# Smaller loads among the last 48 rows, and a hand-written list of operations for the last 24

## The chip, the cores and the metric

The kernel runs on one core of a Trainium2 chip. The metric is the device time of one execution in microseconds (us), as the median of several. A profile of one execution shows what each engine did; its span is some 2 us shorter than the device time. In the profiles PE is TensorE's matmul, PEld its weight load, DVE VectorE, ACT ScalarE, POOL GpSimd, SP the engine that issues the loads.

## The reference

```python
def setup_inputs():
    batch, seq, dim = 32, 512, 1024
    return {"x": np.abs(np.random.randn(batch, seq, dim)).astype(np.float32) + 1e-6}

def reference(x):
    return np.sum(1.0 / x, axis=-1).astype(np.float32)
```

That is 16384 sums of 1024 reciprocals. Each of the 128 partitions has 128 of them; "row 17" below means the 17th sum of every partition, 0.52 MB in all. The input is 67.1 MB.

## The kernel before

For a row with halves a and b, 1/a + 1/b = (a + b)/(a b), so one reciprocal of 512 products replaces 1024 reciprocals. A row passes through these steps:

- **Load** into a ring of 40 rows, with up to eight loads outstanding.
- **Product** a b, on GpSimd for most rows (`pr`). For nine of the 128 rows VectorE does it; TensorE then first copies b to PSUM (`b`).
- **Ln, then Exp** of minus the Ln, on ScalarE.
- **Sum** on VectorE. For half of the rows TensorE has added a + b in PSUM (`s`), and VectorE multiplies 512 elements ("half form", 0.68 us). For the others it multiplies all 1024 elements of the row by the reciprocal, read twice ("full form", 1.22 us).

```python
A, B, C = (2, 0, 0), (2, 2, 0), (2, 2, 1)     # rows, rows with a+b, rows whose product is VectorE's
L, S1 = (1, 0, 0), (1, 1, 0)
LOADS = [[A, B, A, B], [A, B, A, C]] * 5 + [[A, B, A, C]]            # 11 loads of 8 rows
LOADS += [[A, B], [A, C]] * 3 + [[A], [B], [A], [B], [A]]            # 6 of 4, then loads of 2
LOADS += [[L, S1], [S1, S1], [L, S1]]
# ...
for (m, e, v), pr in zip(chunks, made):
    if v < m:
        nc.gpsimd.tensor_tensor(out=pr[:, v:, :], in0=xc[:, v:, :H], in1=xc[:, v:, H:], op=mult)
    # ... TensorE: s = a + b for the first e rows
    if waiting:
        sum_rows(*waiting)                       # VectorE: the chunk before
    nc.scalar.activation(out=pr, in_=pr, func=Ln, scale=S)
    # ... Exp into PSUM (rows without a+b) or in place (rows with a+b)
    waiting = c0 + q, xc, pr, sm, rc
```

Every engine executes its instructions in program order.

## Time and profile before

| | before |
|---|---|
| device time, median | 171.06 us (171.01 to 171.15) |
| span of the profiled run | 169.0 us |
| busiest engines | GpSimd 83%, ScalarE 80%, TensorE 77%, VectorE 72% |
| last load landed | 160.93 us |
| last sum ended | 166.53 us |

No engine is busy throughout. What is nearly never idle is the stream of loads. "Landed" is when the last of the sixteen DMA engines that share a load has reported; the trace records each report. The page lists the loads of the kernel before by size (count, KB each, median us from issue to landing):

```profile
ring<-in_x_dram SPq DMA_DIRECT2D x11, 4096.0 KB, 37.7
ring<-in_x_dram SPq DMA_DIRECT2D x6, 2048.0 KB, 36.8
ring<-in_x_dram SPq DMA_DIRECT2D x8, 1024.0 KB, 28.2
```

The 28 to 38 us are time in the queue: the loads are issued far ahead, so in this trace the stream always has work queued. The time is therefore the stream plus what is left to do after it. The prediction shows the lines of that remainder.

### The profile page before, as it was taken

To read this page: it belongs to the slowest core of one execution; us is meant where nothing else is said; L and a number is where in the kernel's file an instruction comes from. 1 tells how busy PE (TensorE), PEld (TensorE's weight loads), DVE (VectorE), ACT (ScalarE), POOL (GpSimd) and SP (SyncE) were. 2 spreads that over 40 slices of the span, in tenths; PEclk is the share of its full clock that TensorE was granted. 3 is DMA by queue.
4 is the path that set the end of the run, shared out by engine and by line. 5 is a ranking of instruction groups with operands and counts; after the bars stand their busy time and mean duration, and the time that the engine had idled before them with its cause. 6 is when DMAs were issued, how large, how long until landed. Compare 5 with 4: busy or idle time off the path is not lost.

```text
span 169.0 us, 1265 instructions
## 1 busy us (share of the span) xinstructions
PE 130.5 (77%) x274; PEld 49.9 (30%) x274; DVE 121.1 (72%) x265; ACT 134.7 (80%) x135; POOL 140.7 (83%) x73
## 2 busy tenths in 40 slices
PE   0008899786988879875999869798879999997880
PEld 0003333331332233231343323243323433332320
DVE  0000777767987577776787689778789898988784
ACT  3002989978887988958979797898999999999992
POOL 1008999699995999679996998979999999999970
PEclk9999999999999999999699999999999999999999
DMA  6999999999999999999999999999999999999600
GB/s 217 411 457 403 457 411 457 411 457 411 457 405 442 426 442 423 442 421 442 419 450 419 442 426 428 395 426 428 426 434 426 426 415 419 417 426 421 256 0 16
DMA packets 3750, 67.24 MB, mean 398 GB/s; under 512 B 416, under 2 KB 544, under 8 KB 544
## 3 DMA queue, kind: packets, MB, share of 16 engines
q1 hardware_dynamic: 3744, 67.18, 93.3%
q8 instruction: 2, 0.03, 0.1%
q14 instruction: 4, 0.03, 0.0%
HBM read 67.11 MB, written 0.07 MB: 397 GB/s over the span
## 4 chain that ended last, share of the span: by engine, by line
DMA 52%; POOL 22%; ACT 13%; issue 8%; DVE 3%; POOLq 0%; DVEq 0%; SPq 0%
DMA ring<-in_x_dram 52%; POOL pr L144 22%; ACT pr L155 8%; ACT r L160 2%; ACT pr L165 2%; DVE ring L95 2%; DVE pr L95 1%; DVE pr L133 0%; DVE sums L95 0%; POOLq L144 0%; DVEq L198 0%; SPq L125 0%
## 5 line engine op out<-in xcount | busy, mean ns | idle before, releaser
L144 POOL TENSOR_TENSOR pr<-ring 128x1024 f32<-128x1024 f32 (+1 forms) x67 | 140.0, 2130 | 22.6 <-DMA ring<-in_x_dram 22.6
L85 PE MATMUL s<-ring,ident 128*128 128x512 f32 x256 | 122.9, 618 | 34.3 <-DVE sums L95 17.0
L155 ACT ACTIVATE pr<-pr 128x1024 f32<-128x1024 f32 (+1 forms) x67 | 67.9, 1013 | 28.2 <-POOL pr L144 28.2
L85 PEld LDWEIGHTS s<-ring,ident 128*128 128x128 f32 x256 | 46.6, 193 | 107.8 <-issue 60.1
L95 DVE CUSTOM_DVE_ANT_1 pr<-ring,r 128x1024 f32<-128x1024 f32 x31 | 37.9, 1221 | 44.2 <-ACT r L160 44.2
L95 DVE CUSTOM_DVE_ANT_0 pr<-pr,s 128x512 f32<-128x512 f32 x64 | 41.4, 683 | 0.0
L95 DVE CUSTOM_DVE_ANT_1 ring<-ring,r 128x1024 f32<-128x1024 f32 x33 | 40.1, 1217 | 0.6 <-issue 0.6
L165 ACT ACTIVATE pr<-pr 128x1024 f32<-128x1024 f32 (+1 forms) x34 | 34.2, 1007 | 1.1
L160 ACT ACTIVATE r<-pr 128x1024 f32<-128x1024 f32 (+1 forms) x33 | 33.1, 1002 | 1.0
L95 DVE DVE_READ_ACCUMULATOR2_ANT sums<- 128x1 f32 x128 | 10.5, 82 | 0.0
L85 PE MATMUL b<-ring,ident 128*128 128x512 f32 x18 | 10.0, 639 | 0.0
L133 DVE TENSOR_TENSOR pr<-ring,b 128x512 f32<-128x512 f32 x9 | 6.1, 683 | 0.7 <-PE b L85 0.7
L85 PEld LDWEIGHTS b<-ring,ident 128*128 128x128 f32 x18 | 3.4, 205 | 6.2 <-DMA ring<-in_x_dram 4.3
L56 ACT ACT_TABLE_LOAD x1 | 1.3, 1283 | 0.7 <-PEq L187 0.7
masks.py:197 POOL MEMSET ident<- 128x128 f32 x1 | 0.2, 205 | 0.3 <-POOLq L187 0.3
masks.py:199 POOL TENSOR_SCALAR_AFFINE_SELECT ident<-ident 128x128 f32<-128x128 f32 x1 | 0.3, 292 | 0.1
L187 POOL MEMSET const-float32-0.0<- 128x1 f32 x1 | 0.1, 98 | 0.2 <-issue 0.2
L187 POOL MEMSET const-bfloat16-1.0<- 128x1 bf16 x1 | 0.1, 101 | 0.0
L187 POOL MEMSET const-uint8-127<- 128x1 uint8 x1 | 0.1, 101 | 0.0
L187 POOL MEMSET const-float32-1.0<- 128x1 f32 x1 | 0.1, 99 | 0.0
## 6 DMA issues: line engine op xcount, KB each, us to landing
ring<-in_x_dram SPq DMA_DIRECT2D x11, 4096.0 KB, 37.7
ring<-in_x_dram SPq DMA_DIRECT2D x6, 2048.0 KB, 36.8
ring<-in_x_dram SPq DMA_DIRECT2D x8, 1024.0 KB, 28.2
out_dram<-sums SPq DMA_DIRECT2D x1, 64.0 KB, 1.5
```

Of the source, the lines that this page charges most:

```text
L56: nc.scalar.add_instruction(mybir.InstLoadActFuncSet(name=nc.get_next_instruction_name(), act_func_set_id=act_sets.index("natural_log_exp_ ...
L85: i = nc.tensor.matmul(bank, lhsT=ident, rhs=half, start=k == 0, stop=k == len(halves) - 1,)
L95: i = nc.vector.tensor_tensor_reduce(out=row if out is None else out, in0=row, in1=fac, scale=S, scalar=0.0, op0=mult, op1=plus, accum_out ...
L133: i = nc.vector.tensor_tensor(out=pr[:, j, :], in0=xt[:, q + j, :H], in1=b, op=mult)
L144: i = nc.gpsimd.tensor_tensor(out=pr[:, v:, :], in0=xc[:, v:, :H], in1=xc[:, v:, H:], op=mult)
L155: keep(nc.scalar.activation(out=pr, in_=pr, func=Ln, scale=S))
L160: nc.scalar.activation(out=r, in_=pr[:, e:, :], func=Exp, scale=-1.0)
L165: keep(nc.scalar.activation(out=r, in_=r, func=Exp, scale=-1.0))
L187: nc = _bacc.Bacc("TRN2", target_bir_lowering=False, num_devices=1)
```

## The change

The intent is to shorten what follows the stream. Loads become smaller earlier: rows 80 to 87 come in two loads of four instead of one of eight, rows 104 to 111 in twos instead of fours, rows 124 to 127 singly instead of in twos. From row 104 on the loop over chunks gives way to one list, which fixes each engine's order operation by operation. Four products go to VectorE (before: one), and Ln works on pairs of rows where two are ready together, otherwise on single rows, with Exp chosen separately.

```diff
-    L, S1 = (1, 0, 0), (1, 1, 0)
-    LOADS = [[A, B, A, B], [A, B, A, C]] * 5 + [[A, B, A, C]]
-    LOADS += [[A, B], [A, C]] * 3 + [[A], [B], [A], [B], [A]]
-    LOADS += [[L, S1], [S1, S1], [L, S1]]
+    LOADS = [[A, B, A, B], [A, B, A, C]] * 5 + [[A, B], [A, C]] * 3
+    LAST = 104
+    LAST_LOADS = [2] * 10 + [1] * 4
+    ORDER = """
+        P104+ P106 L104+ S109 P107 E104 E105 T104 P108 B109 L106 L107 S107
+        V109 E106 P110+ T105 L108+ E107 S110 T106 E109 P112+ E108 T107 L110+
+        T108 E110 B114 T109 P115 E111 T110 L112+ S114 V114 E112 T111 L114+
+        P116+ S115 T112 E113 E114+ T113 S117 L116 P118+ T114 L117 T115 E116
+        S118 E117 T116 L118+ P120 T117 S119 E118+ D121 L120+ T118 B123 P122
+        T119 E120+ S122 V123 P124 L122 T120 L123 P125 L124 S124 T121 E122 E123
+        P126 T122 E124 S126 T123 L125 P127 L126 T124 E125 S127 E126 T125 L127
+        E127 T126 T127
+    """
 ... the loop over the list: one branch for each letter
```

P is a product on GpSimd, V one on VectorE with a half that B has copied to PSUM, D one on VectorE with both halves from the ring, S the addition a + b on TensorE, L Ln, E Exp, T the sum on VectorE; the number is the row, a plus means this row and the next in one instruction.

## The prediction

> **What bounds the kernel now.** I read the page first, then landings, chain and timeline of the end. From the page:
>
> ```profile
> PE 130.5 (77%) x274; PEld 49.9 (30%) x274; DVE 121.1 (72%) x265; ACT 134.7 (80%) x135; POOL 140.7 (83%) x73
> ...
> DMA  6999999999999999999999999999999999999600
> ```
>
> No engine is busy all the time, but the DMA row is full from the second slice until slice 37 of 40: the input stream sets the time up to its end, and the last three slices (4.2 us each) are work left over after it. So there are two questions: does the stream end sooner or later, and how long is what follows.
>
> The records of when each load had wholly landed answer the first. In mid-kernel an eight-row load lands 9.71 us after the one ahead (4.19 MB, 432 GB/s), a four-row load 4.90 us, a two-row load 2.48 us. Row 79 has landed at 102.03 us, row 87 at 111.75, row 103 at 131.34, and the last load, rows 126 and 127 together, at 160.93. The last sum ends at 166.52 and the span at 169.04. So 5.6 us lie between last landing and last sum, and 2.5 us after it belong to the output transfer and the end of the program, which the change doesn't touch.
>
> The second is in the chain of waits at the end (start, duration, work):
>
> ```profile
> 143.63 1.17 issue
> 144.80 1.33 POOL pr L144
> ...
> 154.12 2.40 POOL pr L144
> 156.52 0.02 issue
> 156.54 1.06 ACT pr L155
> ```
>
> and the groups by form:
>
> ```profile
> L144 POOL TENSOR_TENSOR pr<-ring 128x1024 f32<-128x1024 f32 x52 | 121.7, 2373 | 22.6 <-DMA ring<-in_x_dram 22.6
> L144 POOL TENSOR_TENSOR pr<-ring 128x512 f32<-128x512 f32 x15 | 19.0, 1286 | 0.0
> L155 ACT ACTIVATE pr<-pr 128x1024 f32<-128x1024 f32 x61 | 64.2, 1053 | 28.2 <-POOL pr L144 28.2
> L155 ACT ACTIVATE pr<-pr 128x512 f32<-128x512 f32 x6 | 3.7, 613 | 0.0
> L133 DVE TENSOR_TENSOR pr<-ring,b 128x512 f32<-128x512 f32 x9 | 6.1, 683 | 0.7 <-PE b L85 0.7
> ```
>
> GpSimd's products (L144) fill the chain from 136 to 156 us. Its 22.6 us of idle time are waits for loads, all before 112 us; from 111.88 to 163.91 it never stops. The reason is rows 80 to 87, the last eight-row load: eight rows become ready at once and GpSimd takes 8.3 us over them, so it stays behind the stream until the end. Rows 112 and 113 have landed at 143.59, their product starts at 144.81; row 127 has landed at 160.93, its product ends at 163.91. After that ScalarE and VectorE finish:
>
> ```profile
> 163.32 0.61 ACT L155 ACTIVATE pr<-pr 128x512 f32<-128x512 f32 x1
> 163.96 0.60 ACT L160 ACTIVATE r<-pr 128x512 f32<-128x512 f32 x1
> 164.50 0.61 ACT L155 ACTIVATE pr<-pr 128x512 f32<-128x512 f32 x1
> 165.14 0.63 ACT L165 ACTIVATE pr<-pr 128x512 f32<-128x512 f32 x1
> 165.84 0.08 DVE L95 DVE_READ_ACCUMULATOR2_ANT sums<- 128x1 f32 x1
> 165.84 0.68 DVE L95 CUSTOM_DVE_ANT_0 pr<-pr,s 128x512 f32<-128x512 f32 x1
> ```
>
> Row 127's Ln starts at 164.50, 0.59 us after its product: ScalarE is itself a queue here, without a gap from 158.59 on.
>
> **What the Trainium skill says.** "ScalarE: Activation LUTs", section "What ACT_TABLE_LOAD costs": an ACTIVATE with immediate scale takes 186 ns plus 0.833 ns per element, and neighbours overlap by about 93 ns. That gives 613 ns for 512 elements and 1039 for 1024; the trace has 613 and 1053. In the timeline independent neighbours start 0.53 us apart (one row) or 0.96 (two rows), dependent ones (Exp on its own Ln) 0.65 or 1.08. "DMA: Bandwidth & Descriptors", "Specifications", puts the fabric ceiling at 435 GB/s; the 432 above agrees, so no order of loads makes the stream much faster. "SBUF — State Buffer", "SBUF: two separate sides": a VectorE operation with two SBUF inputs and a GpSimd operation that reads SBUF exclude each other for a whole instruction. Every VectorE product of before reads one factor from PSUM (683 ns in all nine), so this trace doesn't show it; the change brings one such operation, D121.
>
> **The change part by part.**
>
> Loads. Rows 0 to 79 are as before. Rows 80 to 103 come in six loads of four (before: one of eight, four of four), 104 to 123 in ten of two, the last four singly. Fitting time = c + a x rows to 4.90 and 2.48 gives a = 1.21, c = 0.06; to 9.71 and 4.90, a = 1.20, c = 0.09. A one-row load should take 1.27 to 1.29 us. Landings: row 103 at 102.03 + 6 x 4.90 = 131.43; row 123 at + 10 x 2.48 = 156.23; rows 124 to 127 at 157.5, 158.8, 160.1, 161.35. The stream ends 0.4 us later than before, which costs time only where a consumer waits.
>
> GpSimd. Rows 80 to 83 are now there at 106.9 instead of 111.75. GpSimd finishes rows 72 to 79 at 110.8 and goes straight on (before: idle until 111.88). Its 24 rows to 103, nine pairs at a pitch of 2.33 and three singles at 1.24, take 24.7 us: done at 135.5, not 136.6. For rows 104 to 127 it has 20 products instead of 23 (VectorE: 109, 114, 123 with a copied half in PSUM, 121 directly; before only 110): five pairs and ten singles, 5 x 2.33 + 10 x 1.24 = 24.1 us instead of 27.35. With 1.1 + 3.25 us taken off in all from a lag of 1.2 us at row 112, it catches up about there and from then on waits for each landing: P116+ starts at 148.9, P118+ runs 151.37 to 153.75, P124 ends at 158.9, P125 160.2, P126 161.4, P127 162.7 (before 163.91). About 3 us of the saving turn into waiting for the stream.
>
> ScalarE. For these 24 rows seven pair and ten single Ln, three pair and eighteen single Exp: 10 x 0.96 + 28 x 0.53 = 24.4 us, against 18 x 0.96 + 12 x 0.53 = 23.6 before: 0.8 us dearer. It waits for P116+ (151.3), which wipes out all earlier history, and for P118+. From there I place its list end to end:
> - Ln 118-119 at 153.78, Exp 154.86.
> - Ln 120-121 at 155.93. It needs D121: VectorE gets to it about 154.8, is held by P120 (153.85 to 155.14) if the lock acts, and ends about 155.85.
> - Exp 120-121 at 157.0, Ln 122 at 157.97 (product 157.6), Ln 123 at 158.50 (V123 done about 158.1), Ln 124 at 159.03, Exp 122, 123, 124 at 159.56, 160.10, 160.63.
> - Ln 125 at 161.16, Ln 126 at 161.69, Exp 125 at 162.22, Exp 126 at 162.75, Ln 127 at 163.28 (product 162.7), Exp 127 dependent at 163.93, ending 164.56.
>
> So the end hangs on the landing of rows 118 and 119 plus ScalarE's queue; row 127 could be 0.5 us later at no cost.
>
> VectorE. Twelve full-row sums at a pitch of 1.14 us, twelve half-row sums at 0.61, four products at 0.60: 23.4 us within 30 us of stream. After Exp 126 it does row 126 (half form), then row 127 at 164.62, ending 165.30.
>
> Sum: last sum at 165.30 against 166.52, so 1.2 us off. 171.06 - 1.2 = 169.86; I take 169.9.
>
> **The rivals.**
> 1. The stream becomes the bound: if one-row loads cost clearly more than fitted, or the lost eight-row load slows it, row 127 lands after 162. For it: GpSimd has no backlog left, each of the four loads still ends with its slowest engine. Against: the step from four rows to two cost 0.03 us a load, and the queue still holds eight loads. Every microsecond beyond 0.5 then counts: 170.5 to 171.
> 2. ScalarE's extra single instructions or waits between engines eat the gain: the walk above has no slack after Ln 118. Half a dozen waits of 0.1 us make it 170.4. For it: ScalarE was already 9.84 us of 10 busy between 120 and 150 us. Against: before 151 us it now waits for data and starts fresh.
> 3. D121 and P120 collide worse: if VectorE takes the lock first, P120 is pushed back by 0.7 us, and Ln 120 with it: 170.3. If there is no lock, Ln 120 starts 0.1 us sooner: 169.8.
> 4. The whole of GpSimd's 4 us is gained (167.0). Against: row 127 lands at about 161 whatever is done, and product, Ln, Exp and sum in series take 1.29 + 0.61 + 0.60 + 0.68 us plus about 0.2 of hand-over, so nothing under 164.4 is possible for the last sum: 169.0 in all.
>
> **Range and chances.** 169.0 is the floor from rival 4 with a stream as short as before; my walk gives 169.9; delays as in rivals 1 to 3 add 0.4 to 1. A hand walk leaves out small waits more often than it invents them, so the range reaches further up: 169.2 to 170.7. Two per cent faster would need 167.6, below the floor: 0.02. Two per cent slower, 174.5, would need a stall of 4.5 us that I see nowhere: 0.02.
>
> **What would show it.** GpSimd idle ahead of most products from row 112 on, released by the loads; row 127's product ending about 162.7; ScalarE without gaps from about 153.8; the last landing about 161.3; four VectorE products, one of them from two ring halves, starting when a GpSimd product ends; the last sum near 165.3. I am wrong if GpSimd still runs without pause at 150 us, if the last landing is past 162, or if ScalarE pauses over 0.2 us after 155 us.

## The result

| | before | changed |
|---|---|---|
| device time, median of 6 runs | 171.12 us (171.01 to 171.19) | 169.76 us (169.66 to 170.22) |
| span | 169.0 us | 167.9 us |
| last load landed | 160.93 us | 161.46 us |
| GpSimd's last product ended | 163.91 us | 162.88 us |
| ScalarE's last Exp ended | 165.78 us | 164.62 us |
| last sum ended | 166.53 us | 165.44 us |

The ratio is 0.9929 (95% interval 0.9915 to 0.9943), under 1% faster. The last sum came 1.09 us sooner although the last load landed 0.53 us later.

The page of the changed kernel: busy engines, the DMA row, its loads.

```profile
PE 130.8 (78%) x278; PEld 50.5 (30%) x278; DVE 122.8 (73%) x268; ACT 134.1 (80%) x143; POOL 137.7 (82%) x73
...
DMA  6999999999999999999999999999999999999900
...
ring<-in_x_dram SPq DMA_DIRECT2D x10, 4096.0 KB, 37.8
ring<-in_x_dram SPq DMA_DIRECT2D x6, 2048.0 KB, 37.0
ring<-in_x_dram SPq DMA_DIRECT2D x10, 1024.0 KB, 26.0
ring<-in_x_dram SPq DMA_DIRECT2D x4, 512.0 KB, 16.8
```

The shares have hardly moved; averages do not show this change. Its groups of instructions do (busy us, mean ns | idle us before them, released by what):

```profile
L213 POOL TENSOR_TENSOR pr<-ring 128x512 f32<-128x512 f32 (+1 forms) x15 | 24.5, 1648 | 3.0 <-DMA ring<-in_x_dram 2.4
L231 ACT ACTIVATE pr<-pr 128x512 f32<-128x512 f32 (+1 forms) x17 | 13.0, 794 | 1.0 <-DVE pr L222 0.7
L222 DVE TENSOR_TENSOR pr<-ring,bb 128x512 f32<-128x512 f32 x3 | 2.1, 686 | 0.7 <-PE bb L100 0.6
L215 DVE TENSOR_TENSOR pr<-ring 128x512 f32<-128x512 f32 x1 | 0.9, 864 | 0.0
```

L213 is GpSimd's products of the last 24 rows: 24.5 us of work and 3.0 us of waiting, nearly all for loads. Before, GpSimd ran without a pause from 111.88 us to its end. L231 is Ln: ScalarE waited once for VectorE (0.7 us). The chain of waits of the changed kernel, near its end:

```profile
151.60 2.39 POOL pr L213
153.99 0.02 issue
154.01 1.07 ACT pr L231
...
164.84 0.60 DVE pr L110
165.44 0.01 DVE sums L110
```

GpSimd has only one product in this part of the chain, that of rows 118 and 119, started 0.16 us after they landed (151.44). Before, its products filled the chain from 136 to 156 us. From 154.01 on the chain is ScalarE's list, then VectorE's last sums. The timeline of that end:

```profile
163.35 0.61 ACT L231 ACTIVATE pr<-pr 128x512 f32<-128x512 f32 x1
...
163.99 0.63 ACT L237 ACTIVATE pr<-pr 128x512 f32<-128x512 f32 x1
164.15 0.08 DVE L110 DVE_READ_ACCUMULATOR2_ANT sums<- 128x1 f32 x1
164.15 0.68 DVE L110 CUSTOM_DVE_ANT_0 pr<-pr,s 128x512 f32<-128x512 f32 x1
164.76 0.08 DVE L110 DVE_READ_ACCUMULATOR2_ANT sums<- 128x1 f32 x1
164.76 0.68 DVE L110 CUSTOM_DVE_ANT_0 pr<-pr,s 128x512 f32<-128x512 f32 x1
```

Row 127's Exp ends at 164.62; its sum starts 0.14 us later because row 126's is in front. ScalarE and VectorE finish neck and neck.

### The profile page after: what moved, and what is told of

Read it like the earlier page. It is cut to its first block, busy times and chain, and to the rows that moved or that the text cites. A ratio compares the mean times of both kernels' runs of the same rounds, so it can differ in the third digit from the quotient of the medians.

```text
span 167.9 us, 1307 instructions
## 1 busy us (share of the span) xinstructions
PE 130.8 (78%) x278; PEld 50.5 (30%) x278; DVE 122.8 (73%) x268; ACT 134.1 (80%) x143; POOL 137.7 (82%) x73
## 4 chain that ended last, share of the span: by engine, by line
DMA 71%; ACT 11%; POOL 10%; DVE 3%; issue 2%; PE 2%; DVEq 0%; SPq 0%; POOLq 0%; ACTq 0%
DMA ring<-in_x_dram 71%; POOL pr L159 8%; ACT pr L231 5%; ACT pr L237 3%; ACT r L237 2%; POOL pr L213 1%; DVE pr L110 1%; PE s L100 1%; DVE ring L110 1%; ACT pr L170 1%; ACT r L175 1%; PE bb L100 1%; DVE pr L222 0%; DVE sums L110 0%; DVEq L287 0%
## 5 line engine op out<-in xcount | busy, mean ns | idle before, releaser
L159 POOL TENSOR_TENSOR pr<-ring 128x1024 f32<-128x1024 f32 (+1 forms) x52 | 112.7, 2202 | 21.5 <-DMA ring<-in_x_dram 21.5
L170 ACT ACTIVATE pr<-pr 128x1024 f32<-128x1024 f32 x52 | 54.8, 1053 | 26.9 <-POOL pr L159 26.9
L110 DVE CUSTOM_DVE_ANT_1 pr<-ring,r 128x1024 f32<-128x1024 f32 x27 | 33.0, 1221 | 41.4 <-ACT r L175 41.4
L110 DVE CUSTOM_DVE_ANT_1 ring<-ring,r 128x1024 f32<-128x1024 f32 x37 | 44.8, 1217 | 0.2 <-issue 0.2
L180 ACT ACTIVATE pr<-pr 128x1024 f32<-128x1024 f32 x26 | 27.5, 1057 | 0.8
L175 ACT ACTIVATE r<-pr 128x1024 f32<-128x1024 f32 x26 | 26.7, 1028 | 0.8
L213 POOL TENSOR_TENSOR pr<-ring 128x512 f32<-128x512 f32 (+1 forms) x15 | 24.5, 1648 | 3.0 <-DMA ring<-in_x_dram 2.4
L231 ACT ACTIVATE pr<-pr 128x512 f32<-128x512 f32 (+1 forms) x17 | 13.0, 794 | 1.0 <-DVE pr L222 0.7
L237 ACT ACTIVATE pr<-pr 128x512 f32<-128x512 f32 (+1 forms) x10 | 6.9, 704 | 0.1
L237 ACT ACTIVATE r<-pr 128x512 f32<-128x512 f32 (+1 forms) x11 | 6.8, 625 | 0.1
L100 PE MATMUL bb<-ring,ident 128*128 128x512 f32 x6 | 3.2, 622 | 1.3 <-DMA ring<-in_x_dram 1.2
L222 DVE TENSOR_TENSOR pr<-ring,bb 128x512 f32<-128x512 f32 x3 | 2.1, 686 | 0.7 <-PE bb L100 0.6
```

The source lines that it names most:

```text
L100: i = nc.tensor.matmul(bank, lhsT=ident, rhs=half, start=k == 0, stop=k == len(halves) - 1,)
L110: i = nc.vector.tensor_tensor_reduce(out=row if out is None else out, in0=row, in1=fac, scale=S, scalar=0.0, op0=mult, op1=plus, accum_out ...
L159: i = nc.gpsimd.tensor_tensor(out=pr[:, v:, :], in0=xc[:, v:, :H], in1=xc[:, v:, H:], op=mult)
L170: keep(nc.scalar.activation(out=pr, in_=pr, func=Ln, scale=S))
L175: nc.scalar.activation(out=r, in_=pr[:, e:, :], func=Exp, scale=-1.0)
L180: keep(nc.scalar.activation(out=r, in_=r, func=Exp, scale=-1.0))
```

## The experiments

Theory A is the prediction's: GpSimd's backlog is gone, so products follow the landings, and ScalarE's list from the landing of rows 118 and 119 sets the end; it needs the parts of the change together. The rivals say that one part is the gain: the loads, the early start of GpSimd, or the lighter list of GpSimd. Twelve runs were made (eleven kernels, for the changed one ran twice), all with correct results, in rounds beside the kernel before (171.0 to 171.1 us each time).

| run | median us | ratio to before (95%) |
|---|---|---|
| after_again, the changed kernel | 169.76 | 0.9926 (0.9909 to 0.9943) |
| after_2, the same | 169.66 | 0.9918 (0.9905 to 0.9932) |
| pairs_end | 171.30 | 1.0009 (0.9994 to 1.0024) |
| eight_back | 170.16 | 0.9938 (0.9925 to 0.9951) |
| gpsimd_all | 170.92 | 0.9986 (0.9970 to 1.0001) |
| b_all_loads | 171.05 | 1.0004 (0.9989 to 1.0019) |
| list_old_loads | 172.21 | 1.0064 (1.0052 to 1.0076) |
| z_late | 170.31 | 0.9955 (0.9942 to 0.9968) |
| z_early | 169.83 | 0.9925 (0.9914 to 0.9937) |
| direct | 170.20 | 0.9947 (0.9933 to 0.9961) |
| four_mid | 174.81 | 1.0191 (1.0162 to 1.0220) |
| four_mid_gp | 172.29 | 1.0081 (1.0058 to 1.0105) |

### The yardstick

> The changed kernel unaltered, as the yardstick of this batch. Both theories: 169.8 us (169.6 to 170.2), 1.3 us under the kernel before.

> The changed kernel once more, as the yardstick of this batch: 169.8 us (169.6 to 170.2).

169.76 and 169.66. The single runs of the first go from 169.69 to 170.48, and its profile fell on the 170.48: the last load landed at 162.10 and the last sum ended at 166.10, 0.64 and 0.66 us later than in the first profile of the same kernel. So that slow execution was the stream's doing. The fifth and seventh eight-row loads are where it differs: they landed 10.67 and 10.88 us after the load ahead, against 9.86 and 10.69 in the first profile, where an undisturbed load takes 9.71. In the profile of after_2 the seventh took as long as here (10.89) and the fifth 10.06, and the last load landed at 161.44, so most of the 0.64 us came with the fifth load. Every profile here has these two delays, in varying size. Their cause is open, but the packet records hold a candidate: in all fourteen profiles one packet of a DMA queue marked "instruction" starts while the fifth load is in flight (46.98 to 48.08 us; 8 KB, 0.31 to 0.33 us) and another in the seventh (66.0 to 68.2 us; 16 KB, 0.88 to 1.10 us). Later packets of this kind mostly pass without a visible delay, and no run tested it.

### Single-row loads at the end: pairs_end

```diff
-    LAST_LOADS = [2] * 10 + [1] * 4
+    LAST_LOADS = [2] * 12
```

> The changed kernel, but its last four rows come in two loads of two instead of four of one. Theory A (the parts work together: the gain needs each row's product as soon as the row lands, because ScalarE then has an unbroken list to the end): rows 124 and 125 land at 158.9 instead of 157.7 and 159.0, the Ln of row 124 moves from 159.2 to 160.3, and everything after it on ScalarE moves by the same 1.1 us: 170.8 us (170.5 to 171.0). Rival (single-row loads are no help, the gain is GpSimd's lighter list): within 0.2 us of the changed kernel, 169.8.

171.30 us, the whole gain lost: the direction of theory A, and 0.3 us beyond its range. In the trace rows 124 and 125 landed at 158.76, the Ln of row 124 started at 160.23 instead of 159.17, and the last sum ended at 166.50, 1.06 us later than in the changed kernel, which is the expected amount. The Ln of rows 122, 123 and 124, in the changed kernel in one piece, then here that of row 124, waiting for GpSimd:

```profile
158.10 1.70 ACT L231 ACTIVATE pr<-pr 128x512 f32<-128x512 f32 x3
```

```profile
160.23 0.63 ACT L231 ACTIVATE pr<-pr 128x512 f32<-128x512 f32 x1 [1.14 <-POOL pr L213]
```

From the landing of row 124 to the end both kernels take 7.74 us. The stream of this profile was 0.14 us ahead at row 123 (156.28 against 156.42), so at equal streams the difference would be 1.2 us of the 1.5. Most of the rest lies outside the span: device time less span is 2.2 us in these six runs and 1.9 in those of after_again. Why is not shown.

### One large load back: eight_back

```diff
-    LOADS = [[A, B, A, B], [A, B, A, C]] * 5 + [[A, B], [A, C]] * 3
+    LOADS = [[A, B, A, B], [A, B, A, C]] * 5 + [[A, B, A, C]] + [[A, B], [A, C]] * 2
```

> The changed kernel, but rows 80 to 87 come again in one load of eight. Theory A: GpSimd starts row 80 at about 111.9 again and begins the last 24 rows 1.1 us later, at 136.5, but with 20 products instead of 23 it has caught up with the landings by row 116 (148.9), so nothing is left of it at the end: 169.8 us (169.6 to 170.1). Rival (the earlier start of GpSimd is the gain): the 1.1 us come back in full, 170.9.

GpSimd started row 104 at 136.44 instead of 135.41, was level with the landings at row 116 (149.07 against 149.09), and the last sum ended at 165.47 against 165.44. That is theory A to the letter, and the rival's 1.1 us did not come. ScalarE's Ln of row 108 came 0.31 us later, and its wait before rows 118 and 119 shrank from 0.32 us to 0.07: the later start was just absorbed. The median of the timed runs is 170.16, though, 0.06 above the range, and the profile fell on the fastest of the six (169.88). The intervals of this run and of the changed kernel overlap, so up to 0.4 us may be real without a place in the trace. That remainder stays open.

### The products given back to GpSimd: gpsimd_all

```diff
-  ... P108 B109 L106 ... V109 E106 ... B114 T109 P115 ... S114 V114 E112 ...
+  ... P108+ L106 ... E106 ... T109 P114+ ... S114 E112 ...
-  ... P120 T117 ... D121 L120+ T118 B123 P122 T119 E120+ S122 V123 P124 ...
+  ... P120+ T117 ... L120+ T118 P122 T119 E120+ S122 P123 P124 ...
```

> The changed kernel, but all of the last 24 products are GpSimd's again: the four of VectorE and their three copied halves are gone. Theory A: GpSimd needs 4.6 us more, never catches up with the landings after row 108, row 124's product ends at 160.4 instead of 159.1 and row 127's at 164.1 instead of 162.9; the last sum ends 1.2 us later: 170.9 us (170.5 to 171.2). Rival (the loads are the gain, GpSimd has room): within 0.3 us of the changed kernel.

170.92 us, as theory A said. The timeline of GpSimd from 149 us, and its group on the page:

```profile
149.41 14.59 POOL L213 TENSOR_TENSOR pr<-ring 128x1024 f32<-128x1024 f32 x9
...
L213 POOL TENSOR_TENSOR pr<-ring 128x1024 f32<-128x1024 f32 (+1 forms) x16 | 28.6, 1821 | 0.1
```

Nine products in one piece up to 164.00, 0.1 us of idle time in the last 24 rows instead of 3.0. GpSimd's backlog is back and with it the time, although all the small loads are there.

### The loads alone, the list alone: b_all_loads, list_old_loads

```diff
 (b_all_loads, against the kernel before)
-    LOADS = [[A, B, A, B], [A, B, A, C]] * 5 + [[A, B, A, C]]
-    LOADS += [[A, B], [A, C]] * 3 + [[A], [B], [A], [B], [A]]
-    LOADS += [[L, S1], [S1, S1], [L, S1]]
+    LOADS = [[A, B, A, B], [A, B, A, C]] * 5
+    LOADS += [[A, B], [A, C]] * 3 + [[A], [B], [A], [C]] + [[A], [B], [A], [B], [A]]
+    LOADS += [[L, S1], [S1], [S1], [L], [S1]]
 (list_old_loads, against the changed kernel)
-    LOADS = [[A, B, A, B], [A, B, A, C]] * 5 + [[A, B], [A, C]] * 3
-    LAST_LOADS = [2] * 10 + [1] * 4
+    LOADS = [[A, B, A, B], [A, B, A, C]] * 5 + [[A, B, A, C]] + [[A, B], [A, C]] * 2
+    LAST_LOADS = [4] * 2 + [2] * 8
```

> The kernel before with all of the new loads (ten of eight rows, six of four, ten of two, four of one) and none of the new list. Theory A: GpSimd starts 1.1 us earlier and catches up with the landings about row 112, but the six single products after row 121 take 7.4 us while the stream brings those rows in 5, so row 127's product ends at about 163.6 and the time is 170.7 us (170.4 to 170.9). Rival (the loads are the gain): 169.8 to 170.0.

171.05 us: the loads alone bring nothing, and the rival falls. GpSimd did catch up with the landings at row 112 (144.31 for a landing at 144.18), but its six single products ended at 164.20, later than before (163.91). Expected was 163.6: rows 122 and 123 landed 0.38 us later than I had reckoned (156.61 against 156.23), and the first product started 0.13 us after that.

> The changed list of operations with the loads of the kernel before (eleven of eight rows, six of four, eight of two). Theory A: the list alone has the two-row landings at the end, as in the run with the last rows in pairs: 170.7 us (170.4 to 171.0), so the list alone brings a third of the gain at most. Rival (the list is the gain, the loads only tidy up): 169.8.

172.21 us, a miss for both theories: the list alone makes the kernel 1.1 us slower than before. The trace says why. Ln of rows 108 and 109 (ACT L231) in the changed kernel, then in this one; the bracket is ScalarE's idle time before it and what ended it:

```profile
142.78 1.06 ACT L231 ACTIVATE pr<-pr 128x1024 f32<-128x1024 f32 x1 [0.67 <-DVE pr L222]
```

```profile
145.18 1.06 ACT L231 ACTIVATE pr<-pr 128x1024 f32<-128x1024 f32 x1 [1.63 <-DVE pr L222]
```

Row 109's product is VectorE's, and stands in VectorE's order ahead of the sums of rows 105 to 107. With a four-row load row 109 lands at 141.42, not at 139.01. TensorE's two jobs for the row and then the product follow at the same distance in both kernels, 2.99 us after the landing (142.00 and 144.41). So ScalarE resumes 2.4 us later; the last sum ended at 167.81, 2.37 us later. The list is a schedule for one particular sequence of landings. A list written for the old loads was not tried, nor VectorE's four products in the loop over chunks with the new loads; so the runs don't tell how much of the gain needs the order written by hand.

### ScalarE's slack: z_late, z_early

```diff
+  a branch "Z": nc.scalar.activation(out=scratch, in_=a[:, 0, :], func=Exp, scale=-1.0)
 (z_late)   -  ... E120+ S122 ...      +  ... E120+ Z120 S122 ...
 (z_early)  -  ... V109 E106 P110+ ... +  ... V109 E106 Z106 P110+ ...
```

> The changed kernel with one useless single-row Exp more on ScalarE, between the Exp of rows 120-121 and the Ln of row 122; it writes to a tile that nobody reads. Theory A (ScalarE's list is the path from 154 us on): its whole pitch of 0.53 us shows, 0.5 us over the changed kernel (170.3; 0.4 to 0.6). Rival (the end is set by the last landing and GpSimd, or by VectorE's sums, with ScalarE having room): 0.2 us or less.

> The same useless Exp, but before the Ln of rows 108-109, where ScalarE waits 0.67 us for VectorE's product. Theory A: it fits into that wait, 0.0 us (within 0.15) over the changed kernel. Rival (ScalarE's total work sets the end): 0.5 us.

170.31 and 169.83, against 169.76: 0.5 us and nothing, both as theory A said. (The 169.76 is of another batch; the ratios to the kernel before, 0.9955 and 0.9925 against 0.9926, say the same.) One more instruction of ScalarE at 158 us is paid in full; other places after 154 us were not tried. Before row 109's product ScalarE has 0.67 us to spare.

### Products straight from the ring: direct

```diff
-  ... B109 ... V109 ... B114 ... V114 ... B123 ... V123 ...
+  ...          D109 ...          D114 ...          D123 ...
```

> The changed kernel, but VectorE's products of rows 109, 114 and 123 read both halves from the ring, as row 121's does, without the copy of one half to PSUM by TensorE. A product with two inputs from the ring may have to wait while GpSimd multiplies (the changed kernel's one took 0.86 us instead of 0.69). If the two exclude each other: row 123's product or GpSimd's of row 124 is put off by 0.7 to 1.3 us just where ScalarE's list has no slack: 170.3 to 171.0 us, and in the trace each such product ends about 0.6 us after the end of a GpSimd product, or holds one up. If they don't: the four products take 0.69 us wherever they stand, and the time is 169.7 us, because the copies are gone.

170.20 us, 0.5 over the changed kernel of the same rounds (169.66) and 0.1 under the range that I gave for exclusion. The trace settles it. From the timeline, VectorE's product of row 114, its product of row 123, and around the latter GpSimd's products of rows 122, 124 and 125 in one piece, and ScalarE's Ln of row 124:

```profile
147.62 1.21 DVE L215 TENSOR_TENSOR pr<-ring 128x512 f32<-128x512 f32 x1
...
156.93 4.29 POOL L213 TENSOR_TENSOR pr<-ring 128x512 f32<-128x512 f32 x3 [1.21 <-DMA ring<-in_x_dram]
158.15 0.69 DVE L215 TENSOR_TENSOR pr<-ring 128x512 f32<-128x512 f32 x1
160.02 0.63 ACT L231 ACTIVATE pr<-pr 128x512 f32<-128x512 f32 x1 [0.41 <-POOL pr L213]
```

Row 114's product took 1.21 us and ended 0.55 us after GpSimd's product of row 115 (148.28). Rows 109 and 121 ended 0.55 and 0.54 us after the GpSimd product that they met. In the changed kernel row 121's took 0.86 us and ended 0.55 us after row 120's (155.34). Row 123's got in first and took 0.69; GpSimd's product of row 124 right behind it then took 1.75 us instead of 1.28, and ScalarE stood 0.41 us for it, in the stretch without slack. The profile fell on the slowest execution (170.62), with the stream 0.38 us late at row 118; up to the Ln of row 123 ScalarE is 0.37 us behind the changed kernel, from the Ln of row 124 on 0.85. The difference, 0.48 us, is close to the 0.54 by which the medians differ. So each side shuts the other out, as the page "SBUF — State Buffer" of the Trainium skill says ("SBUF: two separate sides"). Note how it looks: the wait is inside the busy time of the instruction and appears in no list of waits.

### Why the list fails on other landings: four_mid, four_mid_gp

```diff
 (both)
-    LAST_LOADS = [2] * 10 + [1] * 4
+    LAST_LOADS = [4] * 2 + [2] * 6 + [1] * 4
 (four_mid_gp, also)
-  ... P108 B109 L106 ... V109 E106 ...
+  ... P108+ L106 ... E106 ...
```

> The changed kernel, but rows 104 to 111 come in two loads of four (as in the kernel before) instead of four of two; the single rows at the end stay. It is to tell why the new list with the old loads was 1.1 us slower than the kernel before. Theory D (the list's order is tied to the landings: VectorE's product of row 109 stands in its queue ahead of the sums of rows 105 to 107, waits for row 109, which then lands at 141.4 instead of 139.0, and holds up VectorE, then ScalarE's Ln of rows 108-109, whose list has only 0.3 us of slack from there to the end): ScalarE resumes at 145.2 instead of 142.8, the last sum is 2.1 us later, 171.9 us (171.6 to 172.2). Rival (the eight-row load and the pairs at the end did it): within 0.3 us of the changed kernel.

174.81 us, 5.05 over the changed kernel (169.76) where theory D said 2.1. The rival (0.3) falls; D has the place right, as the Ln of rows 108 and 109 shows, and the size wrong:

```profile
147.71 1.06 ACT L231 ACTIVATE pr<-pr 128x1024 f32<-128x1024 f32 x1 [5.00 <-DVE pr L222]
```

It started 4.93 us later than in the changed kernel, and row 109 had landed only 2.28 us later (141.29). The rest is TensorE's. Its timeline after that landing, in the changed kernel, in list_old_loads, and in four_mid (the four matmuls that add row 109's halves, then the two that copy one half):

```profile
139.15 1.96 PE L100 MATMUL s<-ring,ident 128*128 128x512 f32 x4 [1.26 <-DMA ring<-in_x_dram]
140.94 1.02 PE L100 MATMUL bb<-ring,ident 128*128 128x512 f32 x2
```

```profile
141.55 1.96 PE L100 MATMUL s<-ring,ident 128*128 128x512 f32 x4 [2.24 <-DVE sums L110]
```

```profile
141.43 3.75 PE L100 MATMUL s<-ring,ident 128*128 128x512 f32 x4 [3.48 <-DMA ring<-in_x_dram]
144.97 1.92 PE L100 MATMUL bb<-ring,ident 128*128 128x512 f32 x2
```

The same work takes 1.8 + 0.9 us more: half speed. The view by stretches confirms it; after the window and its length come busy time and instructions of PE, PEld, DVE, ACT and POOL, the granted clock, and the DMA share and GB/s. First the changed kernel, then four_mid:

```profile
141.40:147.00 5.60, 4.39 (x11) 1.79 (x10) 5.00 (x10) 4.90 (x9) 5.21 (x4) 1.00 1.01 421
```

```profile
141.40:147.00 5.60, 5.57 (x7) 2.51 (x8) 0.67 (x3) 1.31 (x3) 5.58 (x3) 0.50 1.02 423
```

The clock was 0.50. So four_mid pays the late landing (2.3 us) and then a TensorE at half clock (2.7 us), both on the path; its last sum ended at 170.16, 4.72 us later than in the changed kernel.

The Trainium skill, "TensorE: Matmul & The Clock Gate", part 1 on the HAM clock gate, names as the condition for half the clock "after ≥1 idle window (~3.4µs)". The traces agree with the length of the window, and differ in how much of it must be idle. In the fourteen profiles, from the first record of full clock (16 to 20 us) to 163 us, each stretch of half clock lasts 3.41 us or twice that (in four_mid from 140.31 to 147.13), and the stretches of full clock between them are multiples of 3.41 us. So one can lay windows of 3.41 us over each trace and add up in each the time between TensorE's matmuls. Where the clock was full, all ten windows with 2.03 to 3.02 us of idle time were followed by half clock, none with up to 1.83 us was, and of four with 1.90 or 1.91 us two were. What counts is therefore also where a wait falls. The kernel before and the changed kernel both have a wait of 2.25 us at 78.4 us, ahead of the same four matmuls. First TensorE's line and a view by stretches of the kernel before, then the same of the changed kernel:

```profile
80.65 3.31 PE L85 MATMUL s<-ring,ident 128*128 128x512 f32 x4 [2.25 <-DVE sums L95]
81.20:84.50 3.30, 3.30 (x5) 1.34 (x4) 2.30 (x5) 3.07 (x3) 2.90 (x2) 0.50 0.99 427
```

```profile
80.71 1.98 PE L100 MATMUL s<-ring,ident 128*128 128x512 f32 x4 [2.25 <-DVE sums L110]
81.20:84.50 3.30, 3.30 (x8) 1.25 (x7) 2.31 (x5) 3.06 (x3) 2.92 (x2) 1.00 1.01 437
```

In the kernel before the whole wait lies in one window, in the changed kernel a border divides it (1.00 and 1.26 us). In list_old_loads a border divides the 2.24 us too, with 1.60 us ahead of it; its full clock hung on that. This may also be why the executions of four_mid form two groups, four from 174.78 to 175.09 us and two at 173.52 and 173.66: with half clock for one window instead of two they would be faster. The two have no profile, so that is not shown.

> The same loads as four_mid, but row 109's product is GpSimd's, together with row 108's, and VectorE and TensorE have nothing of it in their queues. Theory D: VectorE no longer stops for row 109; GpSimd pays 1.1 us more but Ln of rows 108-109 can start at about 143.9, 1.1 us later than in the changed kernel and not 2.4: 170.6 us (170.3 to 170.9), faster than four_mid although GpSimd has more to do. Rival (GpSimd's load is what counts with these loads): slower than four_mid, 172.5 or more.

172.29 us: 2.5 us faster than four_mid though GpSimd has one row more, as theory D has it against its rival, but 1.4 us above the range. My text was wrong in one point: TensorE still had row 109's addition a + b in its queue, ahead of row 107's. Ln of rows 108 and 109 did start at 143.97, as expected. But TensorE was at half clock again (after 3.49 us of idle time, from 141.10 to 144.51; granted 0.72 over the same stretch), row 107's addition came late, and VectorE waited for it from 144.40 to 146.85. VectorE then ran without a gap for most of the rest, and the last sum ended at 167.74.

## Why the prediction was right

The time on record was 169.9 us; it is 169.76. Taken by its own steps:

**Loads.** The reading that the last three slices of the DMA row are left-over work was loose: the slice before the last two still has 6 tenths of the stream. The sums use the landings, and these hold. Last landing 161.35 predicted, 161.46 found. The one-row loads took 1.23 to 1.28 us, against 1.27 to 1.29 fitted.

**GpSimd.** Row 104's product predicted at about 135.5, found at 135.41; row 127's end 162.7 against 162.88. "About 3 us of the saving turn into waiting for the stream": 3.0 us of idle time on the page. The run gpsimd_all shows that the shed products were needed, pairs_end that the single landings were, and b_all_loads and list_old_loads that neither the loads nor this list gains anything without the other. They are no sum of parts: the gain is that each product starts at its landing, and either half of the change alone leaves a backlog or a wait.

**ScalarE.** Ln of row 118 at 153.78 predicted, 154.01 found; the end 164.56 against 164.62. That the two ends agree to 0.06 us is in part luck: the list started 0.23 us late and took 0.17 us less than reckoned. That the list has no slack at 158 us is shown by z_late. The step that failed is the one before: that ScalarE waits for P116+ and that this "wipes out all earlier history". The product of rows 116 and 117 ended at 151.47 while ScalarE was busy to 151.55, so there was no wait there. ScalarE had run without a break since row 109's product (142.78 to 153.69), and the only slack is the 0.32 us before rows 118 and 119. It cost nothing in the sum. But it hid how much hangs on row 109, and led to the miss on list_old_loads (1.5 us), where row 109 came 2.4 us later. The 0.32 us of slack took up its share, but ScalarE then stood 0.37 us for row 121's product, so 2.37 us reached the end.

**VectorE and D121.** D121 was to be held by P120 and end at about 155.85; it ended at 155.89. The last sum was to start at 164.62 and started at 164.76, behind row 126's: VectorE is a second queue at the end, which the walk had as free.

**Sum.** 1.2 us predicted for the last sum, 1.09 found in the profiles. The measured gain is 1.36 us. Nearly all of it lies inside the span: the median span is 167.85 us in the six runs of the changed kernel and 169.1 to 169.2 in the batches of the kernel before, 1.3 us apart, while the two profiled executions (169.04 and 167.91) are only 1.13 apart. So it is these two profiles that show the gain somewhat small.

**Rivals.** The stream as the bound (1) did not become so in the median; in the one slower execution with a profile it moves the end one for one (after_again). Waits on ScalarE (2) came to less than feared. The collision (3) is real, and direct shows what more of it costs. The full 4 us (4) was out of reach: the last load landed at 161.46.

## What to carry to other kernels

When a kernel is a full stream plus a remainder, work out from the landings what the remainder must be at least; engine shares say nothing about it. Smaller last loads help only if the first engine behind them has no backlog, and a lighter engine helps only if data land in time for it. A fixed order on engines that work in order belongs to one sequence of landings: change the loads and look again at each operation that stands in front of others while waiting for its row, TensorE's included, since a wait there can also halve its clock; here 2.0 us of idle time within one window of 3.41 us always did it.

## What the Trainium skill lacked or had wrong

- "SBUF — State Buffer" has the exclusion of a two-input VectorE operation and GpSimd right, but not how it looks in a profile: VectorE's product of 0.69 us showed as 0.86 and 1.21 us and ended about 0.55 us after GpSimd's, GpSimd's of 1.28 us showed as 1.75, and no list of waits named it.
- "TensorE: Matmul & The Clock Gate" has the length of the window right (3.41 us), but "after ≥1 idle window (~3.4µs)" asks for too much: all ten full-clock windows with 2.03 to 3.02 us of idle time, and two of the four with 1.90 or 1.91 us, were followed by half clock, none with up to 1.83 us.
- "DMA: Bandwidth & Descriptors" gives about 2.0 us of fixed cost for a single transfer, fitted on another path; it has no figure for loads queued one behind the other. Here they cost 9.71, 4.90, 2.48 and 1.23 to 1.28 us for eight, four, two and one row, thus under 0.1 us each beyond the bytes.
- No page has the two delays of 0.1 to 1.2 us that the stream of loads showed at the fifth and seventh load in every profile, each with a packet of an "instruction" queue in flight; whether that is the cause was not tested.
